# The blocks of an in-projection in another order: the scans' queries in the middle, half of the gates last

## The chip, the core and the metric

The kernel runs on one core of one Trainium2 chip. A core has five engines, each with its own queue of instructions: TensorE (PE, matrix products and transposes), VectorE (DVE, elementwise work), ScalarE (ACT, activations, copies and some DMA issues), GpSimd (POOL, elementwise work) and SyncE (SP, which issues most DMAs). The engines take their instructions in the order in which the program was built; waits between them are semaphores. The metric is the device time of one execution in microseconds (us). The kernel before took a median of 1556.46 us in three runs (1555.35 to 1559.38).

## What is computed

One layer of a diffusion transformer for 1024 latent tokens and 256 context tokens of width 1024. After a modulated RMS norm one projection gives all the inputs of two groups of heads; the first is a gated DeltaNet with a forward and a backward scan, the second a neighbourhood attention. Cut to what matters here:

```python
px = modulate(rms_norm(x, norm1_w), sh1, sc1) @ w_in      # latent tokens
pc = modulate(rms_norm(ctx, norm1_w), csh1, csc1) @ w_in  # context tokens
# group A: columns q, k, v (512 each), z (512), a and b (8 each)
qkv = silu(conv5(p[..., :1536]))
q, k = l2_normalize(q) * 128 ** -0.5, l2_normalize(k)
g, beta = -exp(A_log) * softplus(a + dt_bias), sigmoid(b)
o_f, S_f = chunk_gated_delta_rule(q, k, v, g[0], beta[0], S0_f)
o_b, S_b = chunk_gated_delta_rule(rev(q), rev(k), rev(v), rev(g[1]), rev(beta[1]), S0_b)
o = rms_norm(o_f + rev(o_b), out_norm_w) * silu(z)
# group B: columns q, k, v (512 each); q and k with an RMS norm per head of 64
na_x = neighborhood_attention(qx, kx, vx, kc, vc, rpb, rows)
x = x + g1 * (concat(dn_x, na_x) @ w_out)
x = x + g2 * swiglu(modulate(rms_norm(x, norm2_w), sh2, sc2), w_ffn_in, w_ffn_out)
```

The rule works in chunks; each chunk needs the inverse of a unit triangular matrix made of k, beta and the decays, and for the latent chunks the products of q and k times the decays.

## The kernel before

**Precision by parts.** Products of the projection are sums of three: the normed input as `hh + hl` and the weights as `hi + lo`, with hl times lo left out. A weight block is loaded raw by SP (tile `wraw`, one buffer), cast to `whi` or `zhi` by ACT (L199 for a block, L578 for a wide one), and POOL subtracts to give `wlo` or `zlo` (L200, L579).

**Jobs.** The in-projection is a list of jobs (L1011 to L1020), worked one after the other by the loop from L1031. A `Block` is 128 columns of q, k, v (group A) or nq, nk (group B), computed column by column transposed, with the tokens as the moving side: for each of 8 input tiles 9 products (context 256, latent 512 and 512 tokens), 72 in all, or 6 (latent alone, for q and nq), 48 in all, at L403. A `Wide` is 256 columns of nv, or 264 of the gates z with a and b in it, with tokens as rows: for each tile of 128 tokens 24 products (L586) into one bank. Gates are needed for the latent tokens alone, 8 tiles, nv for 10. The columns of z, a and b are 528 together: z half 0 has 264 of the gates, z half 1 the other 248 and the 16 columns of a and b.

The order of the jobs is

k0 k1 k2 k3 z1 | nk0 nk1 nk2 z0 nk3 | nq0 nq1 nq2 q0 | q1 q2 q3 | nv0 v0 nv1 v1 v2 v3 nq3

**What follows a job.** The products of a block end in two or three of four `blk` banks of PSUM. `evac` copies them out: for nq and nk with ACT into a `cacc` tile (L436, two buffers), for q, k and v with ACT into `cr` (L451) and from there on DVE with the five taps of the convolution (L455, L459). `silu` is ACT's Silu (L466) for q, k, v and its squares for q, nq and nk (L469). `norm`, one job later, is for nq and nk a product with a block matrix (L490), Ln (L491) and Exp (L493 for nq, L495 for nk) on ACT, each with its load of an activation table, a scaling on DVE (L498), and the split into two float16 tiles (L503 and L504 for nk, L510 and L511 for nq) that go out by DMA. `finish`, two jobs later, transposes v (L525, scaled on DVE at L529), makes the products k k (L547) and q k (L547) and stores them. The weights of job n+1 are fetched when job n begins (`prefetch`).

**What runs in the background.** Between the products of a job the loop takes steps of generators: `block_inverses` first (the decays at L825 and L838, transposes at L857, then a recurrence of 30 pairs of DVE instructions on the tile N at L867 and L869, the diagonal at L873, 32 transposes back at L879 with ACT's copies at L881, and the DVE steps at L887 and L890), then `preps`: for each of ten chunks in both directions, products of decays (rg on POOL at L939, L949 and L950 on PE), their Exp (e, L953), the products with k k or q k on DVE (L956), and a chain of small products, each with copies behind it (L968, L971, L979, L981, L982). The context's two chunks can be prepared as soon as the inverses are there; the eight latent ones wait until the last q block is finished (`queries`). A second generator, `modulation`, takes steps in the plain blocks: it loads weights (`wad`) through SP, sums them on DVE (L232, L234) and closes each with four small products (L219).

**The end.** When the last job begins, the generators are drained, their tiles are closed, the pool `sp1` (the scans' output `oacc` is its only tile) is opened, and `attention` issues its first loads (`next(fill)`). After the loop the scans start, with steps of the attention (L302, L304, L314, L324) between them. When nv half 1 is done, 64 DMAs copy the attention's values into another order (`vw_d`, at L1083; `values` says at which job).

Of the kernel before, what the change touches and what calls it, by code (L numbers as in the profile page):

```python
# [9 lines left out]
F32 = mybir.dt.float32  # L10
# [78 lines left out]
def hybrid(ctx, tc, a, dbg):  # L89
# [95 lines left out]

    def weights(wp, raws=2):
        def load(src, kt=KT, n=128, lo_engine=pool, raw=None, hi_engine=None):
            given = raw is not None
            if not given:
                raw = wp.tile([128, KT, 132], F32, name="wraw", tag="wraw", bufs=raws)  # L190
# [184 lines left out]
    with ExitStack() as bs:  # L375
        wp = pools(bs, "wpb", "right", 2)
        shift(bs, "hpad", "right", 64)
        hp = pools(bs, "hp", "right")
        load_w = weights(wp, 1)
        early = ExitStack()  # L380
# [181 lines left out]
        class Wide:  # L562


            def __init__(self, kind, half, zp):
                self.kind, self.half, self.zp = kind, half, zp
                self.n = 264 if kind == "z" else 256

            def prefetch(self):
                h2, n = 2 * self.half, self.n // 2  # L570
                src = a["w_z" if self.kind == "z" else "w_nv"]
                self.hi = self.zp().tile([128, KT, 264], F32R, name="zhi", tag="zhi")
                self.lo = self.zp().tile([128, KT, 264], F32R, name="zlo", tag="zlo")
                for i in range(2):
                    raw = wp.tile([128, KT, 132], F32, name="wraw", tag="wraw", bufs=1)
                    r, s = raw[:, :, :n], slice(i * n, i * n + n)
# [13 lines left out]
            def tiles(self):  # L590
                half = self.half
                if self.kind == "nv":
                    for t in range(NCH):
                        p = self.wide(t, 0, 256)
                        vt = cp.tile([128, 264], F32, name="zt", tag="zt", bufs=2)
                        act.copy(vt[:, :256], p[:, :256])
# [3 lines left out]
                if half == 1:  # L600
                    p = bank("blk")
                    for k in range(KT):
                        for j, (ww, x) in enumerate(((self.hi, hh), (self.hi, hl), (self.lo, hh))):
                            pe.matmul(p[:16, :CT], ww[:, k, 248:264], x[k][:, :CT], start=k == 0 and j == 0,
                                      stop=k == KT - 1 and j == 2)
                    abT = cp.tile([16, CT], F32, name="abT", tag="abT")
                    act.copy(abT, p[:16, :CT])
                    yield
                nz = 264 if half == 0 else 248
                for t in range(2, NCH):  # L610
                    p = self.wide(t, 0, 264)
                    if half == 1 and t == 3:
# [3 lines left out]
                        act.copy(ab[:, 0:2].rearrange("p c d -> p (c d)"), q[:, :32])  # L616
                    zt = cp.tile([128, 264], F32, name="zt", tag="zt", bufs=2)
                    act.activation(zt[:, :nz], p[:, :nz], AF.Silu)
                    if half:
                        act.copy(ab[:, t], p[:, 248:264])  # L620
                    act.dma_start(z_d[(t - 2) * 128:(t - 1) * 128, half * 264:half * 264 + nz], zt[:, :nz])
                    yield
# [410 lines left out]
        for n in range(2, len(jobs) + 2):  # L1033
            j = jobs[n] if n < len(jobs) else None
            if n == inv:
# [16 lines left out]
            if isinstance(j, Wide):  # L1052
                for t, _ in enumerate(j.tiles()):
                    next(fin, 0)
                    if t == 4 and nrm:
# [5 lines left out]
                        nrm = None  # L1061
                    if n < turn:
                        bg.step(2)
                    if n >= turn:
                        bg.step(2)
            elif j:
# [37 lines left out]

    oacc = sp1.tile([128, 8, 4, 128], F32, name="oacc", tag="oacc")

# [561 lines left out]
def host(inputs):  # L1668
# [67 lines left out]
```

## Time and profile before

| | us |
|---|---|
| median of three runs | 1556.46 |
| lowest and highest | 1555.35, 1559.38 |
| the profiled execution | 1557.82 |
| its span, first to last instruction | 1556.0 |
| around the span | 1.82 |
| PE busy in it | 1481.6 |
| DVE, ACT, POOL busy | 1003.7, 718.5, 229.1 |
| mean granted clock of TensorE | 0.986 of full |

The profile is of one execution. It has busy times of each engine, groups of instructions by source line, waits by the engine and line that ended them, a timeline of each engine, and windows of time with busy times and the granted clock of TensorE. A timeline line is start, duration, engine, line, operation, output and inputs with their size, and in brackets the idle time ahead of it with what ended it. Matmuls are pipelined, so durations of neighbours overlap. `<-` reads "made from" or, for waits, "released by". Line numbers are those of the kernel before.

### The profile page before, as it was taken

Reading aid. Unit: us, or ns where it says so; the run is one execution under the profiler, and the core shown is the slowest. Engines: PE = TensorE matmul, PEld = TensorE weight load, DVE = VectorE, ACT = ScalarE, POOL = GpSimd, SP = SyncE. Lnnn points to the kernel's source line nnn. Section 1 sums busy time; section 2 is a strip of 40 time slices with the busy share of each in tenths; the row PEclk is TensorE's granted clock in tenths of the full one; section 3 lists DMA queues with packets and bytes.
Section 4 is the critical chain, followed back from the end, with each engine's and each line's share of the span. In section 5 each row is a group of like instructions: output and inputs, shape, how many; then the busy total and the mean of one; then the engine's idle time right before and its main releaser. Section 6 shows DMA issues by size and latency. Waiting matters only on the chain. (4 is left out here: it accounts for less than half of the span.)

```text
span 1556.0 us, 24056 instructions
## 1 busy us (share of the span) xinstructions
PE 1481.6 (95%) x8702; PEld 1234.4 (79%) x8702; DVE 1003.7 (65%) x1856; ACT 718.5 (46%) x1376; POOL 229.1 (15%) x280
## 2 busy tenths in 40 slices
PE   7999999999889988997999999999999999999998
PEld 4788787679888766886788878888888888888887
DVE  5774496573254655678997559855665656689652
ACT  6442554654353355666763266333333334454440
POOL 1154401633354320111100000000000000000000
PEclk9999999999999999999999999999999999999999
DMA  9274221677355568999736601633323224698742
GB/s 391 59 221 125 72 76 61 204 219 212 122 173 157 167 190 251 283 287 262 213 114 227 233 34 53 227 108 106 104 102 102 102 102 156 229 378 283 241 147 81
DMA packets 202422, 267.35 MB, mean 172 GB/s; under 512 B 16832, under 2 KB 112576, under 8 KB 201280
## 3 DMA queue, kind: packets, MB, share of 16 engines
q1 hardware_dynamic: 196688, 261.07, 52.3%
q10 hardware_dynamic: 5616, 4.76, 0.9%
q8 instruction: 68, 1.11, 0.3%
q14 instruction: 50, 0.41, 0.1%
HBM read 201.02 MB, written 68.94 MB: 173 GB/s over the span
## 5 line engine op out<-in xcount | busy, mean ns | idle before, releaser
L403 PE MATMUL blk<-hh,whi 128*128 128x512 f32 (+1 forms) x410 | 122.4, 393 | 1.4 <-ACT kk L548 1.4
L1374 ACT CAST uhi<-wq 128x512 fp32r<-128x512 f32 x101 | 61.1, 622 | 132.2 <-issue 84.9
L1374 ACT CAST uhi<-ws 128x512 fp32r<-128x512 f32 x91 | 53.9, 621 | 146.7 <-PE ps L1313 92.5
L403 PE MATMUL blk<-hh,wlo 128*128 128x512 f32 (+1 forms) x410 | 117.0, 379 | 0.6 <-POOL wlo L200 0.6
L403 PE MATMUL blk<-hl,whi 128*128 128x512 f32 (+1 forms) x410 | 115.3, 376 | 0.3 <-DVE hl L689 0.3
L1375 DVE TENSOR_TENSOR ulo<-wq,uhi 128x512 fp32r<-128x512 f32 x101 | 67.6, 687 | 58.8 <-ACT uhi L1374 33.7
L1313 PE MATMUL ps<-hT,uhi 128*128 128x512 f32 x336 | 103.7, 390 | 0.0
L1313 PE MATMUL ps<-lT,uhi 128*128 128x512 f32 x336 | 103.5, 389 | 0.0
L1313 PE MATMUL ps<-hT,ulo 128*128 128x512 f32 x336 | 103.4, 389 | 0.0
L1313 PE MATMUL ps<-hB,uhi 128*128 128x512 f32 x288 | 89.2, 391 | 0.6 <-ACT hB L1488 0.6
L1313 PE MATMUL ps<-lB,uhi 128*128 128x512 f32 x288 | 88.8, 389 | 0.4 <-DVE lB L1489 0.4
L1313 PE MATMUL ps<-hB,ulo 128*128 128x512 f32 x288 | 88.6, 389 | 0.0
L586 PE MATMUL blk<-zhi,hh 128*128 128x256 f32 (+1 forms) x288 | 84.7, 294 | 1.1 <-ACT kk L548 1.1
L403 PEld LDWEIGHTS blk<-hh,wlo 128*128 128x128 f32 x410 | 72.5, 192 | 15.6 <-POOL wlo L200 0.9
L403 PEld LDWEIGHTS blk<-hl,whi 128*128 128x128 f32 x410 | 72.5, 193 | 14.8 <-DVE hl L689 0.8
L586 PE MATMUL blk<-zhi,hl 128*128 128x256 f32 (+1 forms) x288 | 83.0, 288 | 0.0
L403 PEld LDWEIGHTS blk<-hh,whi 128*128 128x128 f32 x410 | 69.9, 194 | 16.5 <-issue 4.0
L586 PE MATMUL blk<-zlo,hh 128*128 128x256 f32 (+1 forms) x288 | 81.8, 284 | 0.0
L1313 PEld LDWEIGHTS ps<-lT,uhi 128*128 128x128 f32 x336 | 63.1, 188 | 13.2
L1313 PEld LDWEIGHTS ps<-hT,ulo 128*128 128x128 f32 x336 | 63.1, 188 | 13.1
L1313 PEld LDWEIGHTS ps<-hT,uhi 128*128 128x128 f32 x336 | 62.9, 188 | 12.9
L200 POOL TENSOR_TENSOR wlo<-wraw,whi 128x1024 fp32r<-128x1024 f32 x18 | 44.7, 2484 | 183.8 <-ACT whi L199 164.4
(359 smaller groups left out, 3651.6 us busy)
## 6 DMA issues: line engine op xcount, KB each, us to landing
wq<-w_fo SPq DMA_DIRECT2D x99, 256.0 KB, 4.1
wq<-w_gu SPq DMA_DIRECT2D x88, 256.0 KB, 2.9
wad<-wa SPq DMA_DIRECT2D x64, 256.0 KB, 4.0
bt<-rpb SPq DMA_DIRECT2D x64, 192.0 KB, 3.6
t_d<-g SPq DMA_DIRECT2D x22, 512.0 KB, 3.6
fr<-t_d SPq DMA_DIRECT2D x44, 256.0 KB, 5.1
f_d<-g SPq DMA_DIRECT2D x33, 256.0 KB, 2.1
fr<-f_d SPq DMA_DIRECT2D x33, 256.0 KB, 4.3
```

The lines of the kernel that those rows point to most:

```text
L200: lo_engine.tensor_tensor(o, r, h.bitcast(F32), OP.subtract)
L403: pe.matmul(o, ww[:, k], xx[k][:, s], start=k == 0 and j == 0, stop=k == KT - 1 and j == 2)
L586: pe.matmul(p[:, :c1 - c0], x[k][:, s], ww[:, k, c0:c1], start=k == 0 and j == 0, stop=k == KT - 1 and j == 2)
L1313: pe.matmul(o, w[wi][:, k], x[xi][:, k], start=first and k == 0 and j == 0, stop=k == n - 1 and j == 2, skip_group_check=True)
L1374: act.copy(hi, self.raw[key])
L1375: dve.tensor_tensor(lo, self.raw[key], hi.bitcast(F32), OP.subtract)
```

## The change

The order of the jobs becomes

k0 k1 k2 k3 z1 | nk0 nk1 nk2 nk3 nq0 nq1 | q0 q1 q2 q3 | nq2 nq3 nv0 v0 nv1 v1 v2 v3 | z0

- All q blocks stand together behind nq1, `queries` are these four, and nq2 and nq3 come behind them.
- z half 0 is the last job. The split of the columns becomes 256 and 272: half 0 has 256 gates, half 1 has 256 gates and a and b. The host packs two arrays, `w_z0` and `w_z1`; the raw tile is 136 columns wide per half load in place of 132.
- A wide job's hi and lo lie in one tile `zw`. That of z half 0 comes from `sp1`, under the tag that `oacc` has afterwards. So the drain of the generators, the opening of `sp1` and the first loads of the attention come one job before the last, at v3.
- The transposed a and b (`abT`) use a buffer of tag `zt`. `values` still names nv half 1. The two calls of `bg.step(2)` in the loop become one.

```diff
-        load_w = weights(wp, 1)
+        load_w = weights(wp, 1, 136)
...
-                self.n = 264 if kind == "z" else 256
+                self.n = 272 if kind == "z" and half else 256
+                self.lasting = kind == "z" and not half
+
+            def room(self):
+                w = self.zp().tile([128, 2, KT, 256 if self.lasting else 272], F32R, name="zw", tag="zw")
+                self.hi, self.lo = w[:, 0], w[:, 1]
 
             def prefetch(self):
                 h2, n = 2 * self.half, self.n // 2
-                src = a["w_z" if self.kind == "z" else "w_nv"]
-                self.hi = self.zp().tile([128, KT, 264], F32R, name="zhi", tag="zhi")
-                self.lo = self.zp().tile([128, KT, 264], F32R, name="zlo", tag="zlo")
+                src = a["w_nv"] if self.kind == "nv" else a["w_z%d" % self.half]
+                if self.kind == "z":
+                    h2 = 0
+                if not self.lasting:
+                    self.room()
                 for i in range(2):
-                    raw = wp.tile([128, KT, 132], F32, name="wraw", tag="wraw", bufs=1)
+                    raw = wp.tile([128, KT, 136], F32, name="wraw", tag="wraw", bufs=1)
...
-                nz = 264 if half == 0 else 248
                 for t in range(2, NCH):
-                    p = self.wide(t, 0, 264)
+                    p = self.wide(t, 0, self.n)
...
-        jobs += [Block("nk", i) for i in range(3)] + [Wide("z", 0, zp), Block("nk", 3)]
-        jobs += [Block("nq", i) for i in range(3)] + [Block("q", 0)]
+        jobs += [Block("nk", i) for i in range(4)] + [Block("nq", i) for i in range(2)]
         turn = len(jobs)
-        jobs += [Block("q", i) for i in (1, 2, 3)]
+        jobs += [Block("q", i) for i in range(4)]
         later = len(jobs)
-        values = later + 2
-        queries = range(turn - 1, later)
-        jobs += [Wide("nv", 0, zp), Block("v", 0), Wide("nv", 1, zp), Block("v", 1), Block("v", 2), Block("v", 3), Block("nq", 3)]
+        queries = range(turn, later)
+        jobs += [Block("nq", i) for i in (2, 3)]
+        jobs += [Wide("nv", 0, zp), Block("v", 0), Wide("nv", 1, zp), Block("v", 1), Block("v", 2), Block("v", 3)]
+        values = len(jobs) - 4
+        jobs.append(Wide("z", 0, zp))
...
-            if n == len(jobs) - 1:
+            if n == len(jobs) - 2:
                 bg.drain()
                 bg2.drain()
                 late.close()
                 sp1 = pools(middle, "sp1", "left")
+                zpool[0] = sp1
+                jobs[n + 1].room()
                 fill = attention(pools(attn, "nw", "left", 2))
                 next(fill)
...
-    oacc = sp1.tile([128, 8, 4, 128], F32, name="oacc", tag="oacc")
+    oacc = sp1.tile([128, 8, 4, 128], F32, name="oacc", tag="zw")
...
-    o["w_z"] = blocks(w[:, 1536:2064], 132)
+    o["w_z0"] = blocks(w[:, 1536:1792])
+    o["w_z1"] = blocks(w[:, 1792:2064], 136)
```

More of the change, by code (lines that the diff above doesn't have):

```diff
@@ L184, in rsqrt, with weights @@
             dve.scalar_tensor_tensor(r, y, 1.5, r, op0=OP.add, op1=OP.mult)
-    def weights(wp, raws=2):
+    def weights(wp, raws=2, wide=132):
         def load(src, kt=KT, n=128, lo_engine=pool, raw=None, hi_engine=None):
@@ L189, in load @@
             if not given:
-                raw = wp.tile([128, KT, 132], F32, name="wraw", tag="wraw", bufs=raws)
+                raw = wp.tile([128, KT, wide], F32, name="wraw", tag="wraw", bufs=raws)
             hi = wp.tile([128, KT, 128], F32R, name="whi", tag="whi")
@@ L594, in tiles @@
                         p = self.wide(t, 0, 256)
-                        vt = cp.tile([128, 264], F32, name="zt", tag="zt", bufs=2)
+                        vt = cp.tile([128, 272], F32, name="zt", tag="zt", bufs=2)
                         act.copy(vt[:, :256], p[:, :256])
@@ L603, in tiles @@
                         for j, (ww, x) in enumerate(((self.hi, hh), (self.hi, hl), (self.lo, hh))):
-                            pe.matmul(p[:16, :CT], ww[:, k, 248:264], x[k][:, :CT], start=k == 0 and j == 0,
+                            pe.matmul(p[:16, :CT], ww[:, k, 256:272], x[k][:, :CT], start=k == 0 and j == 0,
                                       stop=k == KT - 1 and j == 2)
-                    abT = cp.tile([16, CT], F32, name="abT", tag="abT")
-                    act.copy(abT, p[:16, :CT])
+                    abT = cp.tile([16, 272], F32, name="abT", tag="zt", bufs=2)
+                    act.copy(abT[:, :CT], p[:16, :CT])
                     yield
-                nz = 264 if half == 0 else 248
                 for t in range(2, NCH):
-                    p = self.wide(t, 0, 264)
+                    p = self.wide(t, 0, self.n)
                     if half == 1 and t == 3:
@@ L616, in tiles @@
                         act.copy(ab[:, 0:2].rearrange("p c d -> p (c d)"), q[:, :32])
-                    zt = cp.tile([128, 264], F32, name="zt", tag="zt", bufs=2)
-                    act.activation(zt[:, :nz], p[:, :nz], AF.Silu)
+                    zt = cp.tile([128, 272], F32, name="zt", tag="zt", bufs=2)
+                    act.activation(zt[:, :256], p[:, :256], AF.Silu)
                     if half:
-                        act.copy(ab[:, t], p[:, 248:264])
-                    act.dma_start(z_d[(t - 2) * 128:(t - 1) * 128, half * 264:half * 264 + nz], zt[:, :nz])
+                        act.copy(ab[:, t], p[:, 256:272])
+                    act.dma_start(z_d[(t - 2) * 128:(t - 1) * 128, half * 256:half * 256 + 256], zt[:, :256])
                     yield
@@ L1061, in hybrid @@
                         nrm = None
[L1062 to L1065, printed above, removed]
+                    bg.step(2)
             elif j:
```

## The prediction

> **What bounds the kernel now.** The page was read first: the span, the engines' busy times, and the chain of work that ended last.
>
> ```profile
> span 1556.0 us, 24056 instructions
> PE 1481.6 (95%) x8702; PEld 1234.4 (79%) x8702; DVE 1003.7 (65%) x1856; ACT 718.5 (46%) x1376; POOL 229.1 (15%) x280
> PE 40%; DVE 1%; issue 0%; DVEq 0%
> ```
>
> PE is busy for 95% of the span. The change leaves the number of products alone, so it can only move PE's 74 us of idle time (1556.0 - 1481.6) and the stretches in which PE runs at a low clock. Next came PE's waits from 100 to 700 us, where the in-projection lies, and busy time and granted clock by stretch (columns: length; busy time with instruction counts of PE, PEld, DVE, ACT and POOL; clock; DMA share; GB/s).
>
> ```profile
> PE pr L968 <- DVE y L981: 5.6, 3, 2.6
> PE sc L314 <- DVE bt L309: 4.6, 2, 4.1
> PE m L879 <- DVE N L873: 3.6, 1, 3.6
> ```
>
> ```profile
> 205.00:215.00 10.00, 10.00 (x85) 10.00 (x84) 9.62 (x9) 5.01 (x7) 0.00 (x0) 1.00 0.41 121
> 240.00:250.00 10.00, 10.00 (x45) 7.97 (x44) 9.72 (x9) 3.58 (x5) 2.55 (x1) 1.00 0.18 52
> 250.00:260.00 10.00, 6.38 (x32) 5.12 (x31) 5.27 (x12) 2.99 (x7) 2.38 (x1) 0.83 0.00 0
> 260.00:270.00 10.00, 10.00 (x52) 7.93 (x51) 3.05 (x3) 8.59 (x13) 0.00 (x0) 1.00 0.51 185
> 270.00:280.00 10.00, 10.00 (x44) 7.66 (x44) 9.93 (x9) 6.78 (x8) 4.42 (x5) 1.00 0.66 219
> 282.00:371.00 89.00, 85.48 (x474) 67.86 (x474) 53.27 (x59) 49.22 (x83) 45.67 (x50) 0.94 0.72 211
> 400.00:565.00 165.00, 151.11 (x1162) 128.56 (x1160) 83.27 (x101) 69.26 (x150) 70.41 (x82) 0.96 0.51 159
> 565.00:600.00 35.00, 26.29 (x162) 19.94 (x163) 18.10 (x38) 20.14 (x33) 2.53 (x8) 0.90 0.83 233
> ```
>
> The reader is to see four places. The recurrence on DVE that inverts the blocks stalls PE once, for 3.6 us. The queries (282 to 371) have 89.0 - 85.48 = 3.5 us of idle. The stretch with the latent preparations (400 to 565) has 165.0 - 151.11 = 13.9 us, and at clock 0.96 at most another 0.04 x 165 = 6.6 us. The last block and the first attention step (565 to 600) have 8.7 us and, at 0.90, at most 3.5. Elsewhere PE is full and the change moves nothing.
>
> **What moves, and what it does not cost.** Half 0 of the gates (z0) leaves the place beside the recurrence for the end; all four q blocks stand in the middle, so that the latent preparations, which wait for the last q block, start earlier; nq3 leaves the end. In the order of the built program the first latent L949 stands in the first tile of nv0 (before: in v0) and the last preparation ends in v1 (before: in v3 and nq3). The column split 264+264 into 256+272 keeps the sum of 528, and a wide product is bound by its columns (85 in 10 us of 264 columns): I take 0. Sharing `zt` and `zw` tiles adds no instruction.
>
> **Part 1, the recurrence.** Its rows on PE and DVE:
>
> ```profile
> 250.62 0.61 PE L403 MATMUL blk<-hh,whi 128*128 128x512 f32 x2
> 254.85 0.45 PE L879 MATMUL m<-cst,N 80*128 80x80 f32 x2 [3.62 <-DVE N L873]
> ```
>
> ```profile
> 193.01 0.37 DVE L867 TENSOR_TENSOR tt<-N 80x120 f32<-80x120 f32 x1 [3.77 <-ACT N L859]
> ...
> 255.37 0.28 DVE L869 TENSOR_TENSOR N<-N,tt 80x120 f32<-80x120 f32 x1
> ```
>
> DVE works on N from 193.0 to 255.7. The same norms (nk1, nk2) stand among its steps in both built orders, so its end stays. Beside it PE had z0's 192 wide products (192 x 10/85 = 22.6), nk3's 72 (24 short ones at the wide pace and 48 at 10/45: 13.5) and 44 of nq0 (9.8): 45.9 us. It now has nk3's 72 (13.5) and 144 of nq0, nq1 and q0 (32.0): 45.5. So PE arrives at L879 with about the same 3.6 us to wait. What follows differs. Before, nq blocks were left between the 32 transposes, and PE was full from 254.85 to 280. Now q0 is already done when the wait begins: the order is 24 transposes, 3 of L490 (nk3's norm), 8 transposes, 2 of L490, 4 of L219, and then q1, whose first product needs the `blk` banks that nq1's evacuation (L436) frees. That needs the `cacc` buffer of nk3, hence nk3's whole norm on ACT and DVE, which could not pass N. ACT's durations are these:
>
> ```profile
> 262.28 0.74 ACT L881 COPY WK<-m 128x320 f32<-128x320 f32 x2
> 263.04 1.28 ACT L491 ACT_TABLE_LOAD   x1
> 264.33 1.06 ACT L491 ACTIVATE cr<-m,bias 128x256 f32<-128x256 f32 x2
> 266.65 0.69 ACT L491 ACTIVATE cr<-m,bias 128x512 f32<-128x512 f32 x1 [1.26 <-PE m L490]
> 267.35 1.28 ACT L495 ACT_TABLE_LOAD   x1
> 268.65 1.27 ACT L495 ACTIVATE cr<-cr 128x1280 f32<-128x1280 f32 x1
> 271.54 1.26 ACT L503 CAST hl<-cacc 128x1280 f16<-128x1280 f32 x1 [1.62 <-DVE cacc L498]
> 275.41 1.08 ACT L436 ACTIVATE cacc<-blk 128x512 f32<-128x512 f32 x2
> ...
> 281.33 1.15 ACT L493 ACTIVATE cr<-cr,bias 128x1024 f32<-128x1024 f32 x1
> ```
>
> In ACT's new order from 254.85: six L881 copies at about 0.85 with their transposes (260.0), table load and three L491 (263.4), a copy, table load and L495 (266.4), a copy, table load and two L491 (269.5), L503 (270.8), table load and L493 (273.2), the first half of L436 (273.8). nk3's last DVE step runs beside the last table load. Then q1 issues three products, waits for nq1's square and its L490, and flows from 277.4. From PE's last product, 251.3, that is 26.1 us with some 10.3 us of small work in it (32 transposes, 7 of L490, 4 of L219, 3 of L403): 15.8 us idle in place of 3.6, **+12**. Bounds: 0, if nq1's banks come free without nk3; +22, if all of 254.85 to 277.4 is lost.
>
> The table load took 1.28 us, and the function behind it began 0.01 us after its end, where ACT was already idle of copies (263.02). The Trainium skill, "ScalarE: Activation LUTs", section "What ACT_TABLE_LOAD costs", adds a drain of about 1.38 us to each. By that rule the four loads of this chain would make it 5.5 us longer and the time that much worse; the row shows no such gap, and I use the row.
>
> **Part 2, the queries.** Two context preparations' products run among them. They start after Part 1's stall and meet less filler, with DVE also at q0's and q1's convolutions: **+2** on the row's 3.5 us of idle. Bounds 0 and +8 (idle again as long as all of this stretch's, and its clock loss of 0.06 x 89 = 5.3).
>
> **Part 3, the latent preparations.** Before, they ran among v blocks, and the largest wait was one that a weight load imposed:
>
> ```profile
> 417.66 2.07 PE L968 MATMUL pr<-fx,kk 128*128 128x128 f32 x8 [3.90 <-DVE kk L956]
> ```
>
> ```profile
> 413.59 1.04 ACT L578 CAST zhi<-wraw 128x1024 fp32r<-128x1024 f32 x1 [3.46 <-DMA wraw<-w_nv]
> ```
>
> ACT stood at a cast whose weights had not landed, and e (L953), for which kk and PE wait, stood behind it. The others (L968 <- y) are DVE's convolution ahead of a preparation's copy. Now the steps have a wide tile of 24 products (2.8 us) between them in nv0 and nv1, where DVE has only v0's convolution and the norms of nq2 and nq3 beside them. I count one 3 us wait in nv0, one of about 3.7 in nv1, and 1.4 in v0 and v1: 8.1 in place of 13.9, and half of the clock's 6.6: **-9**. Bounds 0 and -20.5.
>
> **Part 4, z0 at the end.** Its two weight halves go through one raw tile: load on SP, cast on ACT (L578), subtraction on POOL (L579). Rows for the pieces, from 300 to 600:
>
> ```profile
> L578 ACT CAST zhi<-wraw 128x1024 fp32r<-128x1024 f32 x4 | 4.2, 1048 | 12.2 <-DMA wraw<-w_nv 9.5 <-PE blk L586 2.7
> L579 POOL TENSOR_TENSOR zlo<-wraw,zhi 128x1024 fp32r<-128x1024 f32 x4 | 10.3, 2582 | 51.7 <-ACT zhi L578 51.7
> ```
>
> ```profile
> 526.85 1.35 ACT L451 COPY cr<-blk 128x256 f32<-128x256 f32 x3 [5.75 <-PE blk L403]
> ...
> 535.80 1.27 ACT L466 ACTIVATE cacc<-cacc 128x1280 f32<-128x1280 f32 x1
> ```
>
> ```profile
> 527.26 0.35 DVE L455 TENSOR_SCALAR cacc<-cr,cw 128x256 f32<-128x256 f32 x1 [7.46 <-ACT cr L451]
> ...
> 529.23 5.90 DVE L459 SCALAR_TENSOR_TENSOR cacc<-cr,cw,cacc 128x255 f32<-128x255 f32 x6
> ```
>
> In ACT's new order the second cast stands behind v3's copies and v3's Silu (L466). The Silu waits for v3's whole convolution on DVE: as in the v block above, 535.13 - 526.85 = 8.3 us from the first copy, plus v2's scaled copies (L529) between, about 1.8, plus its own 1.27: 11.7 us after v3's last product. Cast and subtraction add 1.05 and 2.58: 15.3. PE has meanwhile 14 transposes of v2 and v3 (about 1.9). The second weight load is no later: the first cast stands behind v2's Silu, some 5 us before v3's last product, and subtraction and load end before v3's Silu does. 15.3 - 1.9 = 13.4, in which the few products that need no zlo run as well: **+13**. Before, nq3's 48 products (10.7 us) covered v3's convolution. Bounds: 0, if another engine order brings the cast forward; +20, if ten of SP's stores (below, 6.9 us) still stand ahead of the second load.
>
> ```profile
> 481.71 34.63 SPq L1083 DMA_DIRECT2D vw_d<-nv_d x50
> ```
>
> Such value stores at 0.69 us each, and 14 attention loads, stand ahead of z0's loads.
>
> Clock: 250 to 260, with the 3.62 us stall, was granted 0.83, a loss of up to 1.7 us, which sits in Part 1's 10.3 of work and is worth as much again here; I leave it in the bounds. The Trainium skill, "TensorE: Matmul & The Clock Gate", Part 1, says the clock is halved after an idle window of about 3.4 us until a busy one has passed. By that, two long stalls cost some 1.7 us each beyond their idle time, 3.4 more in all; the row agrees in size.
>
> **Part 5, the tail.** nq3's norm (two table loads at 1.28, two L491, L493) no longer stands on ACT ahead of the first attention step's Exp, and the second pair's bias loads come earlier; the 4.1 us wait for bt stays in part: **-5** of the 8.7, bounds 0 and -12.2.
>
> Sum: 12 + 2 - 9 + 13 - 5 = **+13**. The profiled execution took 1557.82 (span 1556.0 and 1.82 around it), 1.36 above the median of 1556.46, so the forecast of 1570.8 for it is 1569.5 for the median.
>
> **Rivals.**
> A (not slower): preparations beside wide tiles never starve, so Parts 3 and 5 give back all of 13.9 + 6.6 + 8.7 + 3.5 = 32.7 against losses of 12 + 2 + 13 = 27: -5.7, 1551 to 1554. For it: wide tiles were full while DVE was busy 9.62 of 10 us. Against it: ACT's casts and table loads hold e in any block. It decides from 27 us given back.
> B: only one stall bites, because nq1's evacuation or z0's cast isn't held: 13 - 12 = +1, 1557.5. Against it: both engines take their instructions in the built order.
> C: the stalls come with lower clocks, SP's queue (+7) and +3 in the queries: about +23, 1579.5. For it: row 250 to 260 and the stores.
> D: the preparations do not start earlier. The built order speaks against it; it would add Part 3's 9: 1578.5, and is counted with C.
>
> **How the numbers follow.** Forecast 0.58, A 0.15, B 0.12, C with D 0.15. A change under 0.3% (4.7 us: 1551.8 to 1561.1) can't be told from none. A lies on that bound: 0.08 faster, 0.07 same. B is 0.10 same, 0.02 slower. So faster 0.08, same 0.17, slower 0.75. The forecast's own range is 1562 to 1577. With 1556 to 1582, A's larger part and the upper half of C are left out, about 0.2.
>
> **What would show it.** After: a PE stretch of about 26 us behind the recurrence with under half of it busy, q1's first L403 held by ACT's L436; z0's first wide product held some 13 us by POOL's zlo, behind v3's L466; the 3.90 wait at L968 gone; no L490 after 570. I am wrong if PE is full after the recurrence, or if z0's zlo is ready when v3 ends.

## The result, and the profile after

The changed kernel takes 1574.39 us (median of four, 1570.13 to 1575.41) beside 1555.90 for the kernel before on the same chips (four, 1554.64 to 1559.38): ratio 1.0107, 95% interval [1.0086, 1.0128]. Line numbers of the changed kernel are 6 or 7 higher behind its first edits: L885 is the old L879, L593 the old L586, L974 the old L968.

The page of the changed kernel, and its waits from 100 to 700 us:

```profile
span 1572.9 us, 24070 instructions
PE 1485.7 (94%) x8702; PEld 1239.0 (79%) x8702; DVE 1005.2 (64%) x1856; ACT 715.4 (45%) x1374; POOL 227.8 (14%) x280
```

```profile
PE pr L974 <- DVE kk L962: 9.3, 4, 3.7
PE m L885 <- DVE N L879: 9.1, 1, 9.1
PE m L525 <- ACT cacc L466: 8.5, 1, 8.5
...
PE blk L403 <- ACT cacc L436: 3.7, 1, 3.7
PE sc L314 <- DVE bt L309: 3.3, 2, 3.0
...
PE blk L593 <- POOL zw L586: 1.2, 1, 1.2
```

The span is 16.9 us longer: 12.8 of it is PE's idle time (87.2 in place of 74.4), 4.1 is PE's busy time, with as many products as before. So some products ran slower. Two waits stand out, at the two places where z0 was taken out and put in: 9.1 us for N (3.6 before) and 8.5 us for v3's Silu, which is new. The windows of the changed kernel (columns as before):

```profile
195.27:264.15 68.88, 56.67 (x254) 44.95 (x252) 66.70 (x65) 25.60 (x30) 13.50 (x5) 0.96 0.21 58
254.26:290.00 35.74, 20.68 (x61) 11.76 (x61) 21.93 (x27) 22.32 (x31) 5.19 (x7) 0.62 0.28 89
290.00:381.56 91.56, 87.17 (x533) 72.52 (x531) 60.00 (x76) 43.57 (x77) 44.93 (x49) 0.98 0.75 229
390.00:562.50 172.50, 164.17 (x1300) 143.28 (x1301) 80.40 (x100) 75.13 (x163) 63.98 (x82) 0.97 0.56 172
562.49:576.34 13.85, 3.47 (x20) 2.48 (x17) 9.68 (x14) 3.18 (x4) 2.36 (x1) 0.64 0.58 171
573.00:581.00 8.00, 6.78 (x33) 6.26 (x34) 0.69 (x1) 1.00 (x2) 2.36 (x1) 0.57 0.96 243
```

and the kernel before over its recurrence:

```profile
193.01:255.65 62.64, 57.53 (x349) 49.94 (x347) 60.46 (x65) 26.05 (x34) 5.06 (x2) 1.00 0.19 56
```

PE had about the same work beside the recurrence, 56.7 and 57.5 us; but the recurrence took 68.9 us in place of 62.6. From PE's last product ahead of the wait for N (254.26) to 290, PE was busy for 20.7 of 35.7 us, at 0.62 of its clock. From 390 to v3's end, idle time was 172.50 - 164.17 = 8.3 us. Behind v3 PE stood for 13.85 - 3.47 = 10.4 us, and from 573 to 581 its clock was 0.57. ACT's timeline has the order there, with z0's second cast behind v3's Silu:

```profile
571.64 1.27 ACT L466 ACTIVATE cacc<-cacc 128x1280 f32<-128x1280 f32 x1 [8.17 <-DVE cacc L459]
572.81 1.03 ACT L585 CAST zw<-wraw 128x1024 fp32r<-128x1024 f32 x1
```

Where the time went, by four events that both kernels have: the recurrence's first instruction on DVE and three products. The products' rows, first before, then after, from each kernel's timeline of PE:

```profile
371.22 0.36 PE L586 MATMUL blk<-zhi,hh 128*128 128x256 f32 x1
...
559.20 0.47 PE L403 MATMUL blk<-hh,wlo 128*128 128x512 f32 x1
...
597.30 1.06 PE L1190 MATMUL ps<-v,y 128*128 128x128 f32 x8
```

```profile
381.56 0.68 PE L593 MATMUL blk<-zw,hh 128*128 128x256 f32 x1
...
561.74 0.76 PE L403 MATMUL blk<-hh,wlo 128*128 128x256 f32 x3
...
614.08 2.08 PE L1196 MATMUL ps<-v,y 128*128 128x128 f32 x8
```

These are nv0's first product, v3's last and the scans' first. z0's 192 products (22.6 us) went from the stretch between recurrence and nv0 to the one behind v3, nq3's 48 (10.7) the other way: 11.9 us of work. Smaller work moved too. These rows of the kernel before are examples of it:

```profile
374.16 1.05 PE L547 MATMUL m<-cacc,kTh 128*128 128x128 f32 x8
...
387.32 1.84 PE L484 MATMUL m<-ones,cr 128*128 128x1 f32 x16
...
564.11 0.85 PE L979 MATMUL pr<-y,kk 128*32 128x96 f32 x16
...
577.50 1.98 PE L490 MATMUL m<-cr,cst 128*128 128x512 f32 x4 [0.37 <-ACT cr L469]
```

The last products of q2 and q3 (four such groups of L547 and one of L484) stood beside nv0 and now stand ahead of it: 4.9 us, from the start of each group to the start of the next product. The last preparation's products (five groups of L979, 2.7 us) and nq3's norm (L490, 2.0 us) stood behind v3's last product and now stand ahead of it: 4.6 us. The fourth column has the sums.

| stretch | before | after | work moved | change |
|---|---|---|---|---|
| up to the recurrence | 193.0 | 195.3 | | +2.3 |
| recurrence to nv0 | 178.2 | 186.3 | -7.0 | +15.1 |
| nv0 to v3's last product | 188.5 | 180.9 | -0.3 | -7.3 |
| v3's last product to the scans | 37.6 | 51.6 | +7.3 | +6.7 |
| scans to the end | 958.7 | 958.8 | | +0.1 |

The sum is 16.9. The recurrence began between 191.5 and 195.5 us in all profiled kernels, whatever was changed behind it, so the first line is within what one execution differs from another.

### The profile page after: what moved, and what is told of

It reads as the page before. It is cut to its first block, busy times and chain, and to the rows that moved or that the text cites. A ratio compares the mean times of both kernels' runs of the same rounds, so it can differ in the third digit from the quotient of the medians.

```text
span 1572.9 us, 24070 instructions
## 1 busy us (share of the span) xinstructions
PE 1485.7 (94%) x8702; PEld 1239.0 (79%) x8702; DVE 1005.2 (64%) x1856; ACT 715.4 (45%) x1374; POOL 227.8 (14%) x280
## 5 line engine op out<-in xcount | busy, mean ns | idle before, releaser
L403 PE MATMUL blk<-hh,whi 128*128 128x512 f32 (+1 forms) x410 | 118.1, 383 | 5.1 <-ACT cacc L436 3.7
L593 PE MATMUL blk<-zw,hh 128*128 128x256 f32 (+1 forms) x576 | 116.6, 295 | 1.2 <-POOL zw L586 1.2
L403 PE MATMUL blk<-hl,whi 128*128 128x512 f32 (+1 forms) x410 | 116.2, 375 | 0.3 <-DVE hl L695 0.3
L403 PE MATMUL blk<-hh,wlo 128*128 128x512 f32 (+1 forms) x410 | 113.8, 373 | 0.6 <-POOL wlo L200 0.6
L1381 DVE TENSOR_TENSOR ulo<-wq,uhi 128x512 fp32r<-128x512 f32 x101 | 67.7, 688 | 59.2 <-ACT uhi L1380 32.7
L593 PEld LDWEIGHTS blk<-zw,hh 128*128 128x128 f32 x576 | 94.5, 196 | 3.7 <-POOL zw L586 1.5
L403 PEld LDWEIGHTS blk<-hh,whi 128*128 128x128 f32 x410 | 69.0, 190 | 20.0 <-ACT cacc L436 4.5
L593 PE MATMUL blk<-zw,hl 128*128 128x256 f32 (+1 forms) x288 | 83.8, 291 | 0.0
L403 PEld LDWEIGHTS blk<-hl,whi 128*128 128x128 f32 x410 | 71.7, 189 | 15.2 <-issue 1.0
L403 PEld LDWEIGHTS blk<-hh,wlo 128*128 128x128 f32 x410 | 71.5, 190 | 15.4 <-issue 1.5
```

The source lines that it names most:

```text
L403: pe.matmul(o, ww[:, k], xx[k][:, s], start=k == 0 and j == 0, stop=k == KT - 1 and j == 2)
L593: pe.matmul(p[:, :c1 - c0], x[k][:, s], ww[:, k, c0:c1], start=k == 0 and j == 0, stop=k == KT - 1 and j == 2)
L1381: dve.tensor_tensor(lo, self.raw[key], hi.bitcast(F32), OP.subtract)
```

## The experiments

All edits but the first are to the changed kernel, or to a kernel made from it. Times are medians, ratios are to the kernel before on the same chip. Each interval reaches 2 to 5 us to either side, so a difference of less than about 5 us between two of these kernels isn't shown.

**The queries alone.** The kernel before with

```diff
-        jobs += [Block("nq", i) for i in range(3)] + [Block("q", 0)]
+        jobs += [Block("nq", 0)]
         turn = len(jobs)
-        jobs += [Block("q", i) for i in (1, 2, 3)]
+        jobs += [Block("q", i) for i in range(4)]
...
-        jobs += [Wide("nv", 0, zp), Block("v", 0),
+        jobs += [Block("nq", i) for i in (1, 2)]
+        jobs += [Wide("nv", 0, zp), Block("v", 0),
```

> The kernel before with one part of the change alone: all four q blocks stand behind nq0, nq1 and nq2 behind them, so the latent preparations start in nv0's first tile and end in v1, as in the changed kernel; z0 stays beside the recurrence, nq3 stays last. Theory: the early preparations are a gain of their own, 5 to 9 us (the changed kernel's stretch from its first latent product to v3's end has 8.3 us of idle where the kernel before has 13.9): 1547 to 1551 beside a before of 1556. Rival: the preparations' waits go where the preparations go, and all is within 2 us of before.

1545.99 us, ratio 0.9924 [0.9903, 0.9945]: 11.8 less than before. One part of the change, alone, is faster than both kernels. From its windows and its timeline of SP:

```profile
377.00:537.00 160.00, 150.46 (x1240) 132.05 (x1239) 72.78 (x87) 74.14 (x161) 65.02 (x81) 0.97 0.52 161
```

```profile
537.22 2.30 SPq L991 DMA_DIRECT2D y_d<-y  x4
...
558.12 1.17 SPq L271 DMA_DIRECT2D bt<-rpb  x2
...
559.82 0.90 SPq L271 DMA_DIRECT2D bt<-rpb  x2
```

Idle time in the stretch of the preparations is 9.5 us, near the changed kernel's 8.3. The preparations' last stores leave SP's queue at 540, and both pairs of the attention's bias loads are issued by 561, 12 us ahead of the first score product. In the kernel before the stores stood there until 566, and the second pair's first load came at 578, 2 us ahead of the first score product:

```profile
558.29 8.07 SPq L991 DMA_DIRECT2D y_d<-y  x4
...
578.03 1.85 SPq L271 DMA_DIRECT2D bt<-rpb  x1
```

From its first score product (572.61) to its end this kernel takes 969.4 us, the kernel before (from 580.26) 975.7, the changed one (from 601.94) 971.0. nq3 is still last here. So the shorter tail comes with preparations that end early, not with nq3's norm being out of the way.

**Split and tiles.** The changed kernel's code with that order of jobs.

```diff
-                self.lasting = kind == "z" and not half
+                self.lasting = False
...
-        jobs += [Block("nk", i) for i in range(4)] + [Block("nq", i) for i in range(2)]
+        jobs += [Block("nk", i) for i in range(3)] + [Wide("z", 0, zp), Block("nk", 3), Block("nq", 0)]
...
-        jobs += [Block("nq", i) for i in (2, 3)]
+        jobs += [Block("nq", i) for i in (1, 2)]
...
-        jobs.append(Wide("z", 0, zp))
+        jobs.append(Block("nq", 3))
...
-            if n == len(jobs) - 2:
+            if n == len(jobs) - 1:
```

> The changed kernel's code (256 and 272 columns, one tile for hi and lo, wider raw tile, a and b transposed in a zt buffer) with the order of the run that has the queries in the middle alone: z0 beside the recurrence, nq0 ahead of the q blocks, nq1 and nq2 behind them, nq3 last. Theory: split and tiles cost nothing, and the order is all: 1544 to 1549, as that run (1546). Rival: the tiles cost some microseconds of waiting, since z0's single tile waits for all of z1's: 1550 or more.

1545.69 us, ratio 0.9925 [0.9903, 0.9947]: the same as the run above. 256 and 272 columns, one tile for hi and lo, the wider raw tile and the shared zt buffer cost nothing that these intervals show. The order of the jobs makes the difference.

**nv0 beside the recurrence.**

```diff
-        jobs += [Block("nk", i) for i in range(4)] + [Block("nq", i) for i in range(2)]
+        jobs += [Block("nk", i) for i in range(3)] + [Wide("nv", 0, zp), Block("nk", 3)] + [Block("nq", i) for i in range(2)]
...
-        jobs += [Wide("nv", 0, zp), Block("v", 0),
+        jobs += [Block("v", 0),
```

> The changed kernel with the wide job nv0 moved into the place that z0 left, between nk2 and nk3, beside the recurrence. Theory: what a wide job gave there was 23 to 28 us of PE's work for two subtractions on POOL, both ahead of the recurrence, and blocks left over for the time behind it; with nv0 there the recurrence takes 62 to 63 us again with two long instructions, PE waits at most 4 us for it and has products between the transposes: 12 us less, while the preparations lose a wide job to run beside (3 to 5 us more): 1563 to 1567 where the changed kernel has 1574. Rival: the middle's loss comes from the q blocks standing close behind the recurrence, and 1571 or more stays.

1564.64 us, ratio 1.0040 [1.0025, 1.0054], as the theory had it: z0 is still last, but another wide job has its old place, and some 10 us come back. The recurrence takes 63.2 us, and PE waits 2.9 for it with products left over:

```profile
254.91 0.53 PE L885 MATMUL m<-cst,N 80*128 80x80 f32 x2 [2.90 <-DVE N L879]
255.18 0.77 PE L403 MATMUL blk<-hl,whi 128*128 128x512 f32 x1
```

**No subtractions during the recurrence.** The four blocks whose weights arrive then get no wlo; their products take whi in its place.

```diff
+            if lo_engine is None:
+                return h, h
             lo_engine.tensor_tensor(o, r, h.bitcast(F32), OP.subtract)
...
+                if inv + 3 <= n <= inv + 6:
+                    jobs[n + 1].prefetch(lo_engine=None)
+                else:
+                    jobs[n + 1].prefetch()
```

> The changed kernel without the subtraction for wlo of the four blocks whose weights arrive during the recurrence (their products take whi in its place, so the low part of these weights is left out; the number of products stays). Theory: without POOL's subtractions one long instruction of five is left in the recurrence, which ends 8 us earlier (60 to 61 us long instead of 68.9), PE's wait for it falls from 9.1 to about 1, and the whole chain behind it moves ahead: 1564.5 to 1567.5. Rival: the chain of norms on ACT and DVE takes up the difference, and 1572 or more stays.

1568.54 us, ratio 1.0066 [1.0042, 1.0090]: 5.8 less than the changed kernel, a near miss, since 7 to 10 less was expected. The recurrence takes 63.3 us (194.59 to 257.87), 5.6 less; the remaining subtraction still holds one of its last instructions, and PE still waits 1.46 and 2.44 us for N where about 1 was expected. In the changed kernel POOL's subtractions and DVE's long instructions go together; its timelines of POOL and DVE:

```profile
200.47 2.52 POOL L200 TENSOR_TENSOR wlo<-wraw,whi 128x1024 fp32r<-128x1024 f32 x1 [19.00 <-ACT whi L199]
```

```profile
200.78 2.84 DVE L873 TENSOR_TENSOR tt<-N 80x600 f32<-80x600 f32 x1
203.66 0.78 DVE L875 TENSOR_TENSOR N<-N,tt 80x600 f32<-80x600 f32 x1
```

An operation on the same size takes 0.78 us alone and 2.84 beside POOL's, 2.06 more; it ends 0.63 us after POOL's does. The changed kernel has five such in the recurrence, the kernel before two: 3 x 2.06 = 6.2, which is the whole difference of 68.9 and 62.6. The Trainium skill, "SBUF — State Buffer", section "SBUF: two separate sides", says that DVE and GpSimd share a pair of ports, which one instruction holds to its end while the other fully blocks; these rows agree, but for 0.15 us (a start only at POOL's end would have ended 0.78 behind it).

**The same subtractions on DVE.** As above, but with `prefetch(lo_engine=dve)`.

> The changed kernel with the subtraction for wlo (L200) of the four blocks whose weights arrive during the recurrence moved from POOL to DVE. Theory: a subtraction on POOL (2.5 us) holds the DVE instruction beside it about 2.07 us longer; four of the five long instructions of the recurrence (2.8 to 3.3 us) become short, against three or four subtractions on DVE of 1.2 us each: the recurrence ends 3 to 5 us earlier, and as PE waits 9.1 us for it, the time falls by as much, to 1569.5 to 1571.5. Rival: the recurrence is not what sets the end of this place (ACT's chain of norms is), and the time stays at 1574.

1571.81 us, ratio 1.0083 [1.0056, 1.0110]. The recurrence falls to 67.7 us only: four long instructions are gone, but four subtractions of 1.21 us stand in their place, and DVE then waits for the norms of nk1 and nk2 in its queue (2.24 and 1.04 us). The time's difference from the changed kernel is within the intervals; a miss at the edge of what was expected.

**nq1 in a buffer of its own.**

```diff
-                self.acc = acc = cp.tile([128, T], F32, name="cacc", tag="cacc", bufs=2)
+                held = kind == "nq" and i == 1
+                self.acc = acc = cp.tile([128, T], F32, name="cacc", tag="kx" if held else "cacc", bufs=3 if held else 2)
```

> The changed kernel with nq1's evacuation (L436) going into a buffer of another tag (kx, three of the same size) in place of nk3's cacc, so that it needn't wait for nk3's norm. Theory of the prediction: q1's first products are held by that; the wait of 3.7 us at L403 for L436 goes and PE has q1's products while ACT works on the norms: 3 to 6 us less, 1568.5 to 1571.5. Rival: the wait for the recurrence (9.1 us) and ACT's own order set q1's start, and the time is within 1.5 us of 1574.

1577.54 us, ratio 1.0125 [1.0092, 1.0157]: not faster; that it is slower isn't shown, the two intervals overlap. The wait of 3.7 us is gone, 0.62 is left:

```profile
279.95 0.80 PE L403 MATMUL blk<-hh,whi 128*128 128x512 f32 x1 [0.62 <-ACT cacc L437]
```

but behind the recurrence's end (263.10) the first context preparation comes no earlier (33.4 us, 32.2 in the changed kernel), and nv0 starts later. That nq1's bank was held is so; that freeing it saves 3 to 6 us is not borne out. (The run has a flaw: a buffer of the tag kx is missing to the queries meanwhile, which may take back a gain; this was not tried apart.)

**No norm for nk3.** Its three L490 products, Ln and Exp are left out. The scaling on DVE then takes the squares as they are, made small by a factor.

```diff
-                for s0, n in self.segs:
+                for s0, n in self.segs if (kind, i) != ("nk", 3) else ():
...
-                if kind == "nq":
+                if (kind, i) == ("nk", 3):
+                    pass
+                elif kind == "nq":
...
-                    act.activation(self.r[:, t0:], acc[:, t0:], AF.Square)
+                    act.activation(self.r[:, t0:], acc[:, t0:], AF.Square, scale=1e-3 if (self.kind, self.i) == ("nk", 3) else 1.0)
```

> The changed kernel without the normalising products, Ln and Exp of nk3 (its scaling and split on DVE stay, so nk3's keys are scaled wrongly): nothing of nk3 is left for PE and ACT behind the recurrence, and nq1's evacuation no longer waits for it. Theory: nk3's norm, which stands in ACT's and DVE's queues behind the recurrence, is what delays both the inverses (first context product L949 32.2 us behind the recurrence's end, 26.6 in the kernel before) and q1: with it gone the distance falls to 25 to 28 us, PE has q1's products beside and behind the recurrence, and although DVE's two steps for nk3 move into the recurrence (3 us) the time falls by 7 to 12 us, to 1562 to 1567. Rival: POOL's holds and the missing wide job alone set it, and 1572 or more stays.

1572.07 us, ratio 1.0104 [1.0077, 1.0131]: the mechanism is there, the expected 7 to 12 us are not. The first context product stands 26.7 us behind the recurrence's end (290.38 against 263.67), as in the kernel before (26.6). But the recurrence grows to 71.7 us, since nk3's two steps on DVE now stand in it, PE still waits 8.5 for it, and the time's gain of 2.3 is within the intervals. (In the profiled execution, the fastest of the four at 1567.12, nv0 comes 5.4 us earlier behind the recurrence's start than in the changed kernel, so something like 5 us can't be excluded.)

**36 more products beside the recurrence.**

```diff
+                warm = bank("pr")
+                for i in range(36):
+                    pe.matmul(warm, hh[i % KT][:, :128], hl[i % KT][:, 256:768], start=True, stop=True)
                 U = WK.rearrange("p d u i -> p (d u) i")
```

> The changed kernel with 36 extra products of 512 columns (their result is used by nothing; 8.2 us of PE's time at full clock) beside the recurrence; in the built order they go ahead of 76 products of the blocks, which so stay over for the time behind the recurrence and stand between its transposes. Theory: what the middle lacks is products left over behind the recurrence: the 9.1 us wait shrinks to about 1, the stretch behind it (254 to 290 us with 15 us idle and a granted clock of 0.62) runs at nearly full clock, and in spite of 8.2 us of more work the time falls by 3 to 8 us, to 1566 to 1571. Rival: the chain of norms on ACT sets the end of this place, and the extra work is either hidden (1573 to 1576) or added (1577 or more).

1578.76 us, ratio 1.0153 [1.0132, 1.0175]: the rival's upper case. The granted clock is 0.62 from 260 to 270 us and full from 270 on, and q1 starts at 281.57 in place of 284.06, but PE still waits 6.05 us for N, later waits are longer (12.0 us in all for kk at the old L968, 9.3 in the changed kernel), and nv0 starts 5 us later from the recurrence's start. Of 8.2 us of added work about half shows in the time, so work that nobody needs doesn't pay here.

What goes with the time in the runs without added work is how long after the recurrence's start the first context product (the old L949) comes: 101.1 us in the changed kernel; 88.9 with nv0 beside the recurrence (9.8 us faster), 94.5 without subtractions (5.8 faster), 98.5 with them on DVE (2.6 faster), 98.4 without nk3's norm (2.3 faster), 102.3 with nq1's own buffer (3.2 slower). This goes together; no run tests it apart from the recurrence's length.

**nq3 ahead of z0.**

```diff
-        jobs += [Block("nq", i) for i in (2, 3)]
+        jobs += [Block("nq", 2)]
...
-        jobs.append(Wide("z", 0, zp))
+        jobs += [Block("nq", 3), Wide("z", 0, zp)]
...
-                        done.add(n - 1)
+                        done.update((n - 2, n - 1))
```

> The changed kernel with nq3 moved from behind nq2 to between v3 and z0 (and the last q block counted as finished at the fifth tile of nv0 instead of at its end, so that the preparations start there). Theory: nq3's 48 products cover v3's convolution and Silu and z0's weights; the waits of 8.5 us (L525 for L466) and 1.2 (L593 for L586) go, with some 3 us of low clock: 1560 to 1564 where the changed kernel has 1574. Rival: z0's weights are held by SP's queue and come late anyway: 1570 or more.

1567.95 us, ratio 1.0066 [1.0041, 1.0091]: 6.4 less, between theory and rival. nq3 covers v3's convolution, but z0 waits all the same, as its timelines of PE and ACT show:

```profile
573.32 0.58 PE L593 MATMUL blk<-zw,hh 128*128 128x256 f32 x1 [6.92 <-ACT zw L585]
```

```profile
564.27 1.03 ACT L585 CAST zw<-wraw 128x1024 fp32r<-128x1024 f32 x1
...
572.22 1.04 ACT L585 CAST zw<-wraw 128x1024 fp32r<-128x1024 f32 x1 [1.89 <-DMA wraw<-w_z]
```

The first cast now stands behind nq3's evacuation and squares, and the second half's load can only begin when POOL has read the one raw tile: 8 us from cast to cast. In the changed kernel z0 is held by ACT's order, here by the one raw tile.

**z0 freed from ACT.** Both casts on POOL, v3's transposes behind z0's products.

```diff
-                    act.copy(self.hi[:, :, s], r)
+                    (pool.tensor_copy if self.lasting else act.copy)(self.hi[:, :, s], r)
...
-                    if t == 4 and nrm:
+                    if t == 4 and nrm and not j.lasting:
...
-                        p = bank()
+                        p = bank("blk" if kind == "v" and i == 3 else "m")
```

> The changed kernel with z0's two casts on POOL in place of ACT, so that they don't stand behind Silu, and v3's transposes put behind z0's products. Theory: ACT's order is what holds z0; its second weights land at about 563 us, half a microsecond after v3's last product, and POOL needs 5 us for cast and subtraction: 4 to 5 us of idle in place of 10.4, 1566 to 1569. Rival: DVE and POOL hold each other, the convolution and the subtractions take longer, or SP's queue decides: 1573 or more.

1571.00 us, ratio 1.0088 [1.0066, 1.0109]. The two waits at z0's start are 1.91 and 2.06 us as expected, in place of 8.47 and 1.22, so ACT's order was what held z0. The profiled execution is 5.2 us shorter, about what these waits give; the median falls by 3.4 only, short of the expected 5 to 8, with intervals that overlap. (A wait of 2.35 at L302 stands in the tail now.)

**v3 last.** In the order of the split-and-tiles run, nq3 and v3 change places.

```diff
-        jobs += [..., Block("v", 2), Block("v", 3)]
+        jobs += [..., Block("v", 2), Block("nq", 3)]
...
-        jobs.append(Block("nq", 3))
+        jobs.append(Block("v", 3))
```

> The same run (1546) with nq3 between v2 and v3, so that v3 is last and its convolution, Silu and transposes stand ahead of the first attention step, while nq3's norm doesn't. Theory: v3's convolution takes 8.3 us on DVE and nothing but 40 score products covers it, as with z0 in the changed kernel: 1549 to 1555. Rival: what holds the tail is nq3's norm (two table loads on ACT ahead of the first Exp), and the time falls to 1543 or less.

1553.97 us, ratio 0.9988 [0.9976, 0.9999]: 8 more than with nq3 last. It is the wait at z0's start without z0, from its timeline of PE:

```profile
579.83 2.59 PE L525 MATMUL m<-cst,cacc 128*128 128x128 f32 x10 [9.92 <-ACT cacc L466]
```

In both orders no job's products are ready to cover v3's convolution and Silu. From the first score product to the end the two runs take 970.4 us (nq3 last) and 969.2 (v3 last), so nq3's norm is worth little in the tail.

**Queries first.** In the same order, the q blocks ahead of nq0.

```diff
-        jobs += [Block("nk", i) for i in range(3)] + [Wide("z", 0, zp), Block("nk", 3), Block("nq", 0)]
+        jobs += [Block("nk", i) for i in range(3)] + [Wide("z", 0, zp), Block("nk", 3)]
...
-        jobs += [Block("nq", i) for i in (1, 2)]
+        jobs += [Block("nq", i) for i in range(3)]
```

> The run with the split, the tiles and the queries in the middle (1546) with the q blocks one place further forward, ahead of nq0: the preparations start one to two jobs earlier, beside nq blocks, before nv0. Theory: what helps the preparations is the wide jobs beside them and that they end before v2; starting beside nq blocks adds nothing: 1544 to 1549. Rival: the earlier the better, 1541 or less.

1561.37 us, ratio 1.0032 [1.0017, 1.0048]. Both cases were wrong: this order costs some 16 us. The first latent product comes at 366.0 in place of 376.6, but PE idles more from 290 to 490 (19.4 us, 9.9 in the run above it is made from), with waits that the other run doesn't have, at L547 (3.5 for squares from ACT) and L985 (2.5 for y from DVE). Why the preparations fare so badly beside nq blocks was not taken apart.

## Why the prediction was right

The forecast was +13; the measured medians differ by 18.5 and the profiled executions by 16.9. Its direction, its two places and the gain between them were right. By stretches its terms come out within some 2 us (+14, -9 and +8 against +15.1, -7.3 and +6.7), but the first of them partly by luck.

- **Part 1, the recurrence: right place, wrong make-up.** Parts 1 and 2 together were put at +14 and measure +15.1. The step that failed is "so its end stays", which put this at nothing: I compared the steps in DVE's queue and left out POOL. Three more blocks' weights arrive during the recurrence, and each subtraction holds DVE by 2.06 us. So the recurrence is 6.2 us longer, and PE waits 9.1 us for it, not 3.6. Behind it ACT's chain came in the order that I counted, but from N to PE's even flow (263.34 to 290) it took 26.7 us, not 22.5. That the idle time of the whole place, 35.74 - 20.68 = 15.1 us, is near the forecast's 15.8 is luck: it is 9.1 for N and 6.0 behind it, where the forecast had 3.6 and 12.2. PE's small work there, counted at 10.3 us, took 20.7 with about 1 us of q1's products in it. That fits the clock, which I had left in the bounds at 1.7 us a stall and which was granted at 0.62 over these 35.7 us. No run changes the clock alone, so its price stays open.
- **nq1's bank.** "q1's first product needs the `blk` banks that nq1's evacuation frees" is in the trace (3.69 us at L403 for L436), but the run that removes it gains nothing, and the run without nk3's norm gains little. POOL's subtractions (5.8 us) and the missing wide job (some 10, with nv0 in its place, these subtractions among them) are what the runs show. What share of the rest is the clock's, and what the late inverses', stays open.
- **Part 2, the queries: not seen.** The 3.69 us wait of the first context product for kk at 303 us belongs to it, but from 290 to nv0 PE idled for 91.56 - 87.17 = 4.4 us (3.5 in the row of before), at a clock of 0.98 in place of 0.94. So there is no +2 here, rather a small gain, which hides part of what Part 1 had too small. (Part 2's upper bound, 3.5 and 5.3, adds up to 8.8, not 8.)
- **Part 3, the preparations: right.** Waits of 8.3 us in place of 13.9 (forecast 8.1), 7.3 us gained (forecast 9), and the 3.90 wait at L968 gone. The half of the clock's loss that I had counted as won didn't come: the clock was 0.97 in place of 0.96. The queries alone gain 11.8 with the tail.
- **Part 4, z0's start: right.** From v3's last product to the first score product (580.26 before, 601.94 after) the time grew by 11.6 us beyond the work moved, forecast 13. The second cast began 10.3 us behind v3's last product (forecast 11.7, though its pieces, 8.3 and 1.8 and 1.27, make 11.4), zlo was there at 13.8 (forecast 15.3), PE idled for 10.4 (forecast 13.4) and then ran 8 us at 0.57. The wait is put down to v3's transposes, which stand ahead of z0's products and need the same Silu; I had counted them as work.
- **Part 5, the tail: right size, wrong cause.** From the first score product to the end it is 4.8 us less (forecast 5). I named nq3's norm; with nq3 still last the tail is 6.3 shorter, and between the two runs of one order with nq3 last and v3 last it differs by 1.2. SP's rows point to the preparations' stores; no run moves them alone.
- **What is left over.** Between the changed kernel and the run with split and tiles lie some 29 us. Mended one at a time, the middle gives back 9.8 (nv0 beside the recurrence) and the end 6.4 (nq3 ahead of z0). No run mends both without moving z0 back, so the rest isn't taken apart.
- **The rivals.** A asked that wide jobs end all waits of the preparations; 8.3 us were left. B fell with both stalls seen. C named the clocks as what could make it worse, and the measured 1574 lies between the forecast and C. D fell with the first latent product at 384.8 in place of 408.6.

## What to carry to other kernels

A reorder that helps one stage is priced at every place that a moved job leaves or enters, and its parts are run alone: here the queries gain 11.8 us, and the rest of the change, z0's move above all, costs more than twice that. A wide job beside a long chain on DVE was worth more here than its products, since its weights come with few subtractions on POOL during the chain; count other engines' instructions during a chain, not the chain's own alone. The job behind the last convolution should have weights that need neither the engine nor the raw tile that the convolution's end holds; the fastest orders here leave z0 beside the recurrence and nq3 last.

## What the hardware showed unasked

A DVE instruction of two inputs beside a POOL subtraction ended 0.63 us behind POOL's end: 2.84 us in place of 0.78. And after one stall the clock stayed low through busy time. These are rows of 2 us of the changed kernel:

```profile
258.00:260.00 2.00, 0.00 (x0) 0.00 (x0) 1.90 (x3) 0.00 (x0) 0.00 (x0) 0.77 0.57 172
...
266.00:268.00 2.00, 2.00 (x14) 1.55 (x12) 0.00 (x0) 1.35 (x4) 0.00 (x0) 0.50 0.00 0
268.00:270.00 2.00, 2.00 (x4) 1.05 (x4) 0.00 (x0) 1.97 (x3) 0.00 (x0) 0.50 0.00 0
270.00:272.00 2.00, 2.00 (x3) 0.81 (x3) 0.00 (x0) 0.83 (x2) 0.00 (x0) 0.50 0.00 0
272.00:274.00 2.00, 1.67 (x10) 1.20 (x9) 0.00 (x0) 1.43 (x3) 0.00 (x0) 0.82 0.00 0
274.00:276.00 2.00, 0.86 (x2) 0.03 (x1) 0.00 (x0) 1.99 (x2) 1.97 (x5) 1.00 0.03 8
276.00:278.00 2.00, 1.50 (x2) 0.50 (x2) 1.83 (x2) 1.97 (x4) 0.87 (x2) 0.54 0.38 154
...
286.00:288.00 2.00, 2.00 (x3) 0.81 (x3) 2.00 (x3) 1.98 (x5) 0.00 (x0) 0.50 0.13 30
288.00:290.00 2.00, 2.00 (x5) 0.99 (x4) 2.00 (x3) 1.99 (x3) 0.00 (x0) 0.55 0.97 309
290.00:292.00 2.00, 2.00 (x10) 1.64 (x9) 0.54 (x1) 1.97 (x3) 0.73 (x1) 1.00 0.95 366
```

From 264 to 272 PE was busy for 7.8 of 8 us, with transposes and the norms' products, and the granted clock was 0.50 all the while. It was full for a short stretch around 274, and behind a wait of 1.64 us (up to 276.50) it was 0.50 again until shortly before 290. The Trainium skill, "TensorE: Matmul & The Clock Gate", Part 1, says half rate after an idle window of about 3.4 us and full rate after a busy one; the rows agree with the two rates, but here the full rate came back only after some 8 us of busy time, and went again behind a shorter wait. Whether the kind of work matters, transposes here, no run tests.
